# A PEER layer on Trainium2: 128 of 512 tokens take their experts by indirect row loads

## The chip, the cores and the metric

The kernel runs on one core of a Trainium2 chip, as one launch. Its time is the device time of that core in microseconds, the median of several runs. The core's engines work side by side, each through its own list of instructions in order: TensorE (PE) for matmuls, VectorE (DVE) for element-wise work, ScalarE (ACT) for activations and copies, GpSimd (POOL) for slower element-wise work and for indirect DMAs, SyncE (SP), which only issues DMAs here. Semaphores join them.

## The reference, cut to what matters

Two transformer blocks in float32, model width 1024. In the first block each of 2 layers has a mixer and then a PEER layer; layer 0 runs PEER on 256 tokens of `x` and 256 of `ctx` (512), layer 1 on 256. A token scores two sets of 128 sub-keys for each of 8 heads, keeps the best 16 of each, and of the 256 sums the best 16: 128 experts a token, out of 16384. The second block (2 layers of feed-forward, mixer, feed-forward on 256 tokens) follows.

```python
s = einsum('chpd,hpnd->chpn', q, sub_keys); s_top, i_top = top_k(s, 16)
cand = s_top[:, :, 0, :, None] + s_top[:, :, 1, None, :]      # and ids i*128 + j
best, pos = top_k(cand, 16); eid = take(cand_id, pos); gate = softmax(best)
u = take(u_tab, eid)                                          # rows of 1024
act = gelu(einsum('chkd,cd->chk', u, hc)) * gate
v = take(v_tab, eid)
return einsum('chk,chkd->cd', act, v)
```

## The kernel before

PEER is computed densely: every token is multiplied with all 16384 rows of the u-table, and all entries but a token's 128 get the gate 0. Both tables come as 128 **pieces** of 128 x 1024 floats (512 KB): SP loads one into `raw` (4 buffers), ACT copies it to `wh` in the fp32r format (L338), and DVE subtracts to get the rest `wl` (L339); where `self.share` is set, every third piece of layer 0 has that subtraction on POOL. A product is three matmuls, wh·xh, wh·xl, wl·xh (`mm3`, L370 to L372), so a piece costs 24 matmuls of 128 x 128 weights against all 512 tokens.

`peer(0)` has two stages. In the **up stage** the u-pieces run through PE (`ublock`, 4 pieces a block), ACT applies gelu (L1169), and the result goes to DRAM (`ad`). Woven into it, `topk` chooses the experts, a tile of 128 tokens after the other: scores on PE (L987), top 16 on DVE (L995 to L999), the candidates' top 16 (L1031 to L1035), 128 selecting steps `cj` (L1050), and then the gates are spread over the 16384 columns by one-hot matrices: `oa` and `ob` on DVE (L1085, L1095), a matmul into `sc` (L1106), an ACT copy (L1111), a POOL addition into `stg` (L1113), a DMA to `gd`. A loop hands `topk` 3.5 units of budget for each u-piece.

In the **down stage** `prep` loads a block of gates and of activations (`g`, `a`, 1 MB each, L1206 and L1211), DVE multiplies them (L1215) and splits them (`w4h`, `w4l`), and the v-pieces multiply them, in 16 groups of two blocks with 8 outputs `d` each; `ev` (L1222) adds the output from PSUM to the residual `xt` on DVE, 128 times. After each `ev` one `sums_step` (L432) prepares a modulation row of later layers: a 512 KB load `arow` and a DVE pass over 128 x 1024 that sums (L442). 48 rows `wmodt` (16 of them are summed twice) and 72 rows `adat` are treated here. `bias_write` (L1398) writes a table `dd` by two DMAs that POOL issues. Layer 1 repeats both stages on 256 tokens, with groups of four blocks and no sums.

A scheduler simulates the program and sets each engine's order from priorities; `topk` runs at a raised one. So the order is not written in the code but follows from it.

## Time and profile before

| | |
|---|---|
| median of 3 runs | 4311.34 us (4310.23 to 4319.42) |
| profiled execution | 4310.78 us |
| its span | 4308.9 us |
| granted TensorE clock, mean | 0.969 |
| busy: PE, DVE, ACT, POOL | 94%, 71%, 43%, 16% |
| up stage of layer 0 | 517 to 1333 us |
| down stage of layer 0 | 1333 to 2084 us |
| up and down stage of layer 1 | 2356 to 2772, 2772 to 3187 us |

The busy share tells how long an engine held an instruction, averaged over stages that have different limits. So the table gives the stretches of the four PEER stages, and the rows further down give what each engine does in each of them. In a timeline the engine's instructions overlap a little at their ends; the distance from start to start is what one more of them costs.

### The profile page before, as it was taken

What the parts mean: (1) busy time and instruction counts of PE and PEld (TensorE: products, weight loads), DVE (VectorE), ACT (ScalarE), POOL (GpSimd) and SP (SyncE); (2) the same over time, 40 slices, a digit from 0 to 9 for tenths busy, and PEclk for the clock granted to TensorE, in tenths of its full rate; (3) what the DMA queues carried; (4) which work ended last, traced back from release to release, by engine and by line L of the source; (5) the groups of instructions that cost most, each with busy time, mean ns of one, the idle gap of its engine ahead of it and who ended that gap; (6) DMA issues with size and microseconds to landing.
All of it is one profiled execution on the core that took longest, in us unless ns stands there. A gap on an engine that the chain in (4) does not pass through costs nothing.

```text
span 4308.9 us, 68836 instructions
## 1 busy us (share of the span) xinstructions
PE 4066.0 (94%) x25534; PEld 3593.9 (83%) x25534; DVE 3048.2 (71%) x7720; ACT 1851.1 (43%) x3052; POOL 690.5 (16%) x612
## 2 busy tenths in 40 slices
PE   7899999999997899999988999999989989999898
PEld 5568788888885688888768999999989879998798
DVE  4754586878776887787676989676658778656764
ACT  3342344444443232322344565544444454444643
POOL 0100024333342000000020476400000110101100
PEclk9999999999998999999999999999999999999999
DMA  5423246454559988786324577887659628564344
GB/s 175 164 72 98 93 134 194 158 184 147 187 171 233 312 291 295 278 299 216 104 65 167 191 259 239 280 308 260 223 178 313 214 94 288 178 195 152 99 161 142
DMA packets 309551, 841.63 MB, mean 195 GB/s; under 512 B 26672, under 2 KB 130736, under 8 KB 296672
## 3 DMA queue, kind: packets, MB, share of 16 engines
q1 hardware_dynamic: 200480, 735.51, 50.0%
q10 hardware_dynamic: 107328, 98.57, 7.0%
q0 software_dynamic: 1408, 3.15, 1.1%
q8 instruction: 202, 3.31, 0.3%
q14 instruction: 133, 1.09, 0.1%
HBM read 734.38 MB, written 102.75 MB: 194 GB/s over the span
## 4 chain that ended last, share of the span: by engine, by line
PE 51%; issue 7%; DVE 7%; DMA 2%; ACT 1%; POOL 1%; ACTq 0%; DVEq 0%; POOLq 0%
PE mm L370 16%; PE mm L371 16%; PE mm L372 16%; DMA a<-ad 2%; DVE wl L339 1%; DVE cj L1050 1%; PE sc L1106 1%; DVE cacc L769 0%; ACT wh L338 0%; DVE nu L534 0%; PE sc L509 0%; PE sc L698 0%; PE nm L708 0%; ACTq L1192 0%; DVE a L1215 0%
## 5 line engine op out<-in xcount | busy, mean ns | idle before, releaser
L338 ACT ACTIVATE wh<-raw 128x1024 fp32r<-128x1024 f32 x946 | 999.6, 1058 | 1819.1 <-PE mm L371 1377.8
L339 DVE TENSOR_TENSOR wl<-raw,wh 128x1024 fp32r<-128x1024 f32 x839 | 1042.9, 1246 | 596.0 <-ACT wh L338 594.4
L372 PE MATMUL mm<-h2h,wl 128*128 128x512 f32 (+1 forms) x2176 | 736.0, 339 | 6.2 <-DVE wl L339 6.1
L370 PE MATMUL mm<-h2h,wh 128*128 128x512 f32 (+1 forms) x2176 | 733.5, 338 | 2.7 <-ACT h2h L539 2.2
L371 PE MATMUL mm<-h2l,wh 128*128 128x512 f32 (+1 forms) x2176 | 735.6, 338 | 0.0
L370 PE MATMUL mm<-w4h,wh 128*128 128x512 f32 (+1 forms) x2048 | 691.6, 340 | 36.5 <-ACT wh L338 18.8
L371 PE MATMUL mm<-w4l,wh 128*128 128x512 f32 (+1 forms) x2048 | 690.5, 339 | 4.1 <-DVE w4l L339 4.1
L372 PE MATMUL mm<-w4h,wl 128*128 128x512 f32 (+1 forms) x2048 | 662.6, 339 | 4.1 <-DVE wl L339 4.0
L370 PE MATMUL mm<-h,wh 128*128 128x256 f32 x1712 | 498.7, 291 | 16.5 <-ACT h L539 6.7
L371 PE MATMUL mm<-h,wh 128*128 128x256 f32 x1712 | 494.6, 289 | 2.4 <-DVE h L540 1.8
L372 PE MATMUL mm<-h,wl 128*128 128x256 f32 x1712 | 491.0, 287 | 0.5 <-DVE wl L339 0.5
L370 PEld LDWEIGHTS mm<-w4h,wh 128*128 128x128 f32 x2048 | 391.8, 192 | 84.9 <-ACT wh L338 27.2
L372 PEld LDWEIGHTS mm<-h2h,wl 128*128 128x128 f32 x2176 | 414.4, 191 | 48.8 <-DVE wl L339 9.4
L370 PEld LDWEIGHTS mm<-h2h,wh 128*128 128x128 f32 x2176 | 414.5, 191 | 45.3 <-ACT h2h L539 2.8
L371 PEld LDWEIGHTS mm<-h2l,wh 128*128 128x128 f32 x2176 | 414.7, 191 | 40.6
L371 PEld LDWEIGHTS mm<-w4l,wh 128*128 128x128 f32 x2048 | 392.1, 192 | 47.2 <-DVE w4l L339 6.5
L372 PEld LDWEIGHTS mm<-w4h,wl 128*128 128x128 f32 x2048 | 388.9, 192 | 47.7 <-DVE wl L339 7.4
L1095 DVE SCALAR_TENSOR_TENSOR ob<-io,top,ix 128x256 fp32r<-128x256 f32 x768 | 322.3, 475 | 145.9 <-PE sc L1106 144.7
L370 PEld LDWEIGHTS mm<-h,wh 128*128 128x128 f32 x1712 | 335.8, 196 | 24.4 <-ACT h L539 10.7
L1113 POOL TENSOR_TENSOR stg<-s 128x256 f32<-128x256 f32 x384 | 312.6, 844 | 228.4 <-ACT s L1111 220.1
L339 POOL TENSOR_TENSOR wl<-raw,wh 128x1024 fp32r<-128x1024 f32 x107 | 263.1, 2459 | 505.7 <-ACT wh L338 444.7
L371 PEld LDWEIGHTS mm<-h,wh 128*128 128x128 f32 x1712 | 335.4, 196 | 9.8 <-DVE h L540 7.1
(339 smaller groups left out, 6809.0 us busy)
## 6 DMA issues: line engine op xcount, KB each, us to landing
raw<-in_ut SPq DMA_DIRECT2D x256, 512.0 KB, 3.9
raw<-in_vt SPq DMA_DIRECT2D x256, 512.0 KB, 4.9
raw<-in_wgu SPq DMA_DIRECT2D x176, 512.0 KB, 4.3
arow<-in_adat SPq DMA_DIRECT2D x144, 512.0 KB, 4.9
gd<-stg ACTq DMA_DIRECT2D x24, 2048.0 KB, 11.2
raw<-in_wdn SPq DMA_DIRECT2D x88, 512.0 KB, 4.3
raw<-in_win SPq DMA_DIRECT2D x66, 512.0 KB, 3.7
ad<-a ACTq DMA_DIRECT2D x32, 1024.0 KB, 4.2
```

The lines of the kernel that those rows point to most:

```text
L338: self.nc.scalar.activation(h, src, AF.Copy)
L339: (eng or self.nc.vector).tensor_sub(l, src, h.bitcast(F32))
L370: mm(out, wh, xh, start=start, stop=False)
L371: mm(out, wh, xl, start=False, stop=False)
L372: mm(out, wl, xh, start=False, stop=stop)
L1050: nc.vector.scalar_tensor_tensor(junk, self.iota[:, :NCAND], pf[:, h, k : k + 1], eid[:, h, :], op0=OP.is_equal, op1=OP.mult, accum_out=se ...
L1095: nc.vector.scalar_tensor_tensor(ob[:, j], iota.unsqueeze(1).to_broadcast([P, 2, P]), ij[:, 1, t : t + 1], ghl[:, t].unsqueeze(2).to_broad ...
L1106: nc.tensor.matmul(pg[:, j * 256 : (j + 1) * 256], oa[:, 2 * h + j], obs[h][:, j].rearrange("p a b -> p (a b)"), start=True, stop=True,)
L1113: nc.gpsimd.tensor_tensor(stg[:, :, c : c + 2].rearrange("p b t -> p t b"), both[:, :, 0], both[:, :, 1], op=OP.add)
```

## The change

Of layer 0, tile 0 (the first 128 tokens, `rows_at(0)`) no longer goes through the dense passes. Its `topk` stops once the expert ids and gates are known (`keep`): the one-hot part is made for three tiles only. 128 **indirect loads** on POOL's queue (`fetch`: each takes, for each of 128 tokens, the 4 KB row of one of its experts, 512 KB in all) bring u-rows into 3 buffers `ur`, and a DVE pass over 128 x 1024 multiplies each with the tokens' input, transposed into PSUM (`xg`), and sums (`rows_up`, 1.17 rows a u-piece once the ids are there). In the down stage 128 more loads bring v-rows into 4 buffers `vr`, each scaled and added to `racc` by one DVE pass (`rows_down`, 1.15 rows an `ev`); at the end 8 PE transposes put the sum into `xt`. The dense matmuls of layer 0, `gd`, `ad` and the steps on them run on `nd` = 384 columns.

With it go: PSUM buffers `mm` 4 to 2 (the transposed input takes two banks); the sub-keys, no longer resident, are loaded as two `raw` pieces for each `topk` tile; the budget 3.5 becomes 3.05; the u-loop of layer 0 runs all 32 blocks in the up stage; the 72 `adat` sums move from the down stage of layer 0 to that of layer 1 (1.25 for each of its 64 `ev`), and the 48 `wmodt` rows stay at 0.42 an `ev`.

```diff
-    a["sk"] = sk.reshape(L, P, 8, 256)
+    a["sk"] = sk.reshape(L, P, 2, 8, P).transpose(0, 2, 1, 3, 4)
+    a["ug"], a["vg"] = i["u_tab"][0], i["v_tab"][0]
...
-    rate = {("gate", 0): (10, 0, 2), ("gate", 1): (4, 0, 2), ("u", 0): 0, ("u", 1): 0, ("v", 0): 1, ("v", 1): 0, "ffn": 1.4, "out": 1, "att": (0.4, 0.4), "norm": ((4,4), (2,2), (4,4), (4,4))}
-
-
-    def topk(self, l, tt, tp, qT, sk, gd):
+    rate = {("gate", 0): (10, 0, 2), ("gate", 1): (4, 0, 2), ("u", 0): 0, ("u", 1): 0, ("v", 0): 0.42, ("v", 1): 1.25, "up": 1.17, "down": 1.15, "ffn": 1.4, "out": 1, "att": (0.4, 0.4), "norm": ((4,4), (2,2), (4,4), (4,4))}
...
+            if hp % 2 == 0:
+                sk = self.raw(self.A["sk"][l, hp // 2]).rearrange("p (a b) c -> p a (b c)", a=4)
...
+        if keep is not None:
+            nc.vector.tensor_copy(keep["id"], sel.rearrange("p h k -> p (h k)"))
+            nc.vector.tensor_copy(keep["gate"], gate.rearrange("p h k -> p (h k)"))
+            keep["ready"] = True
+            return
...
+    def rows_at(self, l):
+        return P if l == 0 else 0
+    def fetch(self, pool, tag, bufs, table, ids, i):
+        r = self.t(pool, [P, D], tag, bufs=bufs)
+        self.nc.gpsimd.indirect_dma_start(
+            out=r, out_offset=None, in_=self.A[table], in_offset=bass.IndirectOffsetOnAxis(ap=ids[:, i : i + 1], axis=0)
+        )
+        return r
+    def rows_up(self, pool, dst, x):
+        todo = []
+        for i in range(P + 2):
+            if i < P:
+                todo.append(self.fetch(pool, "ur", 3, "ug", dst["id"], i))
+            if i >= 2:
+                r = todo.pop(0)
+                self.nc.vector.scalar_tensor_tensor(
+                    r, r, 1.0, x, op0=OP.mult, op1=OP.mult, accum_out=dst["dot"][:, i - 2 : i - 1]
+                )
+                yield
+        a = dst["dot"]
+        self.nc.scalar.activation(a, a, AF.Gelu_apprx_tanh)
+        self.nc.vector.tensor_tensor(a, a, dst["gate"], op=OP.mult)
+    def rows_down(self, pool, dst, acc):
+        todo = []
+        for i in range(P + 3):
+            if i < P:
+                todo.append(self.fetch(pool, "vr", 4, "vg", dst["id"], i))
+            if i >= 3:
+                r = todo.pop(0)
+                c = dst["dot"][:, i - 3 : i - 2]
+                if i == 3:
+                    self.nc.vector.tensor_scalar(acc, r, c, None, op0=OP.mult)
+                else:
+                    self.nc.vector.scalar_tensor_tensor(acc, r, c, acc, op0=OP.mult, op1=OP.add)
+                yield
...
-            es.enter_context(self.banks(mm=4, sc=3, io=1))
+            es.enter_context(self.banks(mm=2 if g0 else 4, sc=3, io=1))
...
+                if g0:
+                    rhs = (lambda k: h2h[:, k, g0:], lambda k: h2l[:, k, g0:])
+                    x = self.t(self.psum, [P, D], "xg", bufs=1)
+                    for k in range(8):
+                        for n, h in enumerate((h2h, h2l)):
+                            nc.tensor.matmul(
+                                x[:, k * P : (k + 1) * P], h[:, k, 0:g0].bitcast(F32), self.ident, start=n == 0, stop=n == 1
+                            )
...
-                while not done and nb < 32:
+                while nb < 32 and not (done and not g0):
...
+                        if g0 and "ready" in dst:
+                            if up is None:
+                                up = self.rows_up(tp, dst, x)
+                                steps = 0
+                            steps += self.rate["up"]
+                            while steps >= 1:
+                                steps -= 1
+                                next(up, None)
...
+                for _ in up or ():
                     pass
...
-                        cols = slice(s * T, s * T + T)
+                        cols = slice(max(g0, s * T), s * T + T)
                         add = nc.vector.scalar_tensor_tensor(
-                            self.xt[:, d, cols], ps[:, cols], mod[:, 40 + d, s : s + 1], self.xt[:, d, cols],
+                            self.xt[:, d, cols], ps[:, cols.start - g0 : cols.stop - g0], mod[:, 40 + d, s : s + 1], self.xt[:, d, cols],
...
+                    if g0:
+                        self.steps += self.rate["down"]
+                        while self.steps >= 1:
+                            self.steps -= 1
+                            with self.tc.issue_after(add.ins):
+                                next(down, None)
...
-                        vp, 4, (0, 1, 2),
-                        (*self.sums_of("wmodt", 0, self.mod1[1], "b_mod1", lambda m: (0, 1) if m < 16 else (0,)),
-                         *self.sums_of("adat", 0, self.mod2[0], "ada_b0", lambda m: (2,))),
+                        vp, 4, (0, 1), self.sums_of("wmodt", 0, self.mod1[1], "b_mod1", lambda m: (0, 1) if m < 16 else (0,))
                     )
+                else:
+                    self.sums_begin(vp, 3, (2,), self.sums_of("adat", 0, self.mod2[0], "ada_b0", lambda m: (2,)))
+                if g0:
+                    acc = self.t(vp, [P, D], "racc")
+                    down = self.rows_down(vp, dst, acc)
+                    self.steps = 0
...
+                    if g0 and i + deep == 32:
+                        rows_end()
...
-                            self.mm3(ps[:, :nt], wh, wl, gh[:, kk], gl[:, kk], k == 0, k == 4 * deep - 1)
-                        ev(d, ps[:, :nt], i + deep == 32)
+                            self.mm3(ps[:, :nd], wh, wl, gh[:, kk], gl[:, kk], k == 0, k == 4 * deep - 1)
+                        ev(d, ps[:, :nd], i + deep == 32)
...
-        self.peer(0, 3.5)
+        self.peer(0, 3.05)
```

Three places of the order. First VectorE, where the selection of tile 0 ends in the up stage (`cj` is the last selecting step; `si`, `idx`, `pf`, `best` lead into the one-hot part; `rowid` holds the ids), before:

```order
L1050 SCALAR_TENSOR_TENSOR cj_1047_4924,sel_894_4475<-io_774_3646,pf_893_4473,eid_875_4311 128x50
L339 TENSOR_TENSOR wl_942_4592<-raw_940_4589,wh_941_4591 128x1024
L1057 CAST si_1048_4926<-sel_894_4475 128x128
L1060 TENSOR_SCALAR idx_1049_4928<-si_1048_4926 128x128
L1061 TENSOR_SCALAR idx_1049_4928<-si_1048_4926 128x128
L1064 CAST pf_1050_4931<-idx_1049_4928 128x128
L1065 CAST best_1051_4932<-idx_1049_4928 128x128
L1085 TENSOR_TENSOR oa_1062_4980<-io_774_3646,top_1053_4939 128x512
L1075 TENSOR_TENSOR ix_1055_4942<-sc_1052_4935,gh_1054_4941 128x128
L1095 SCALAR_TENSOR_TENSOR ob_1063_4982<-io_774_3646,top_1053_4939,ix_1055_4942 128x256 x2
L1095 SCALAR_TENSOR_TENSOR ob_1064_4985<-io_774_3646,top_1053_4939,ix_1055_4942 128x256 x2
L1085 TENSOR_TENSOR oa_1065_4988<-io_774_3646,top_1053_4939 128x512
```

and now:

```order
L1053 SCALAR_TENSOR_TENSOR cj_1061_5012,sel_903_4529<-io_774_3646,pf_902_4527,eid_884_4365 128x50
L1060 CAST rowid_775_3651<-sel_903_4529 128x128
L1151 SCALAR_TENSOR_TENSOR ur_1075_5081,rowdot_777_3653<-ur_1075_5081,xg_841_4013 128x1024
L340 TENSOR_TENSOR wl_1024_4888<-raw_1022_4885,wh_1023_4887 128x1024
L1151 SCALAR_TENSOR_TENSOR ur_1076_5083,rowdot_777_3653<-ur_1076_5083,xg_841_4013 128x1024
L1151 SCALAR_TENSOR_TENSOR ur_1077_5085,rowdot_777_3653<-ur_1077_5085,xg_841_4013 128x1024
L340 TENSOR_TENSOR wl_1045_4954<-raw_1043_4951,wh_1044_4953 128x1024
L1151 SCALAR_TENSOR_TENSOR ur_1082_5135,rowdot_777_3653<-ur_1082_5135,xg_841_4013 128x1024
L1151 SCALAR_TENSOR_TENSOR ur_1087_5185,rowdot_777_3653<-ur_1087_5185,xg_841_4013 128x1024
L998 MAX top_1073_5069<-s_1066_5048 128x8 x8
```

Where the one-hot steps followed, 128 row passes begin, right behind the ids; a `wl` stands between them, and the selection of the next tile begins with the MAX row.

Second GpSimd, where the up stage ends and the down stage begins, before:

```order
L1113 TENSOR_TENSOR stg_2525_11640<-s_2410_11098 128x2x128 x9
L1113 TENSOR_TENSOR stg_2583_11916<-s_2410_11098 128x2x128 x16
L1398 DMA dd_2888_13732<-bv0_2890_13735 1024x1x383
L1398 DMA dd_2888_13732<-bv1_2892_13740 1024x1x383
L846 MEMSET u_3507_17737 128x2x15
```

and now:

```order
L1121 TENSOR_TENSOR stg_2537_11674<-s_2345_10779 128x2x128 x16
L1138 DMA vr_2652_12252<-in_vg,rowid_775_3651 128x1024
L1138 DMA vr_2653_12254<-in_vg,rowid_775_3651 128x1024
L1138 DMA vr_2654_12256<-in_vg,rowid_775_3651 128x1024
L1138 DMA vr_2655_12258<-in_vg,rowid_775_3651 128x1024
L1495 DMA dd_2867_13585<-bv0_2869_13588 1024x1x383
L1495 DMA dd_2867_13585<-bv1_2871_13593 1024x1x383
L1138 DMA vr_2657_12288<-in_vg,rowid_775_3651 128x1024
L1138 DMA vr_2666_12332<-in_vg,rowid_775_3651 128x1024
L1138 DMA vr_2668_12362<-in_vg,rowid_775_3651 128x1024
L1138 DMA vr_2677_12406<-in_vg,rowid_775_3651 128x1024
```

The two writes of `dd` now have four loads of v-rows ahead of them and the other 124 behind them on one queue.

Third VectorE in the middle of the down stage, where before the sums `arow` fill the places between the `ev` (L1222):

```order
L1222 SCALAR_TENSOR_TENSOR xt_4_72<-mm_2923_13960,mod1_0_12_87,xt_4_72 128x256 x2
L442 SCALAR_TENSOR_TENSOR arow_2912_13885,mod1_1_13_88<-arow_2912_13885,crow0_2655_12305 128x1024
L1222 SCALAR_TENSOR_TENSOR xt_4_72<-mm_2931_14003,mod1_0_12_87,xt_4_72 128x256 x2
L442 SCALAR_TENSOR_TENSOR arow_2920_13927,mod1_1_13_88<-arow_2920_13927,crow0_2655_12305 128x1024
L339 TENSOR_TENSOR wl_2947_14091<-raw_2945_14088,wh_2946_14090 128x1024
L448 TENSOR_TENSOR mod1_1_13_88<-mod1_1_13_88,vecs_2_67 128x4
L339 TENSOR_TENSOR w4l_2939_14054<-a4_2940_14055,w4h_2938_14053 128x512 x4
L1215 TENSOR_TENSOR a4_2984_14363<-a4_2984_14363,g4_2981_14359 128x512 x4
L339 TENSOR_TENSOR wl_2954_14145<-raw_2952_14142,wh_2953_14144 128x1024
L1222 SCALAR_TENSOR_TENSOR xt_4_72<-mm_2941_14069,mod1_0_12_87,xt_4_72 128x256 x2
```

and now:

```order
L340 TENSOR_TENSOR wl_2910_13830<-raw_2908_13827,wh_2909_13829 128x1024
L1292 SCALAR_TENSOR_TENSOR xt_4_72<-mm_2897_13754,mod1_0_12_87,xt_4_72 128x128
L1292 SCALAR_TENSOR_TENSOR xt_4_72<-mm_2897_13754,mod1_0_12_87,xt_4_72 128x256
L1170 SCALAR_TENSOR_TENSOR racc_2625_12132<-vr_2884_13673,rowdot_777_3653,racc_2625_12132 128x1024
L1292 SCALAR_TENSOR_TENSOR xt_4_72<-mm_2905_13796,mod1_0_12_87,xt_4_72 128x128
L1292 SCALAR_TENSOR_TENSOR xt_4_72<-mm_2905_13796,mod1_0_12_87,xt_4_72 128x256
L1170 SCALAR_TENSOR_TENSOR racc_2625_12132<-vr_2892_13715,rowdot_777_3653,racc_2625_12132 128x1024
L340 TENSOR_TENSOR wl_2913_13848<-raw_2911_13845,wh_2912_13847 128x1024
L340 TENSOR_TENSOR wl_2930_13943<-raw_2928_13940,wh_2929_13942 128x1024
L340 TENSOR_TENSOR w4l_2921_13906<-a4_2922_13907,w4h_2920_13905 128x384 x2
```

A row pass stands where the sum stood; `ev` adds the second half of `x` and all of `ctx` (128 and 256 columns).

## Rows read from the trace of the kernel before

**Rows 1.** Chain that ended last: share of the span by engine

```profile
PE 51%; issue 7%; DVE 7%; DMA 2%; ACT 1%; POOL 1%; ACTq 0%; DVEq 0%; POOLq 0%
```

**Rows 2.** Windows: PE, PEld, DVE, ACT, POOL busy (instructions); clock, DMA share, GB/s

```profile
517.00:1333.00 816.00, 806.61 (x3771) 672.64 (x3769) 616.92 (x2634) 358.34 (x564) 298.27 (x298) 1.00 0.52 171
1333.00:2084.00 751.00, 712.45 (x3058) 577.79 (x3059) 571.46 (x953) 210.82 (x272) 2.55 (x4) 0.97 0.80 267
...
2772.00:3187.00 415.00, 411.42 (x3404) 411.02 (x3403) 282.14 (x465) 196.59 (x292) 0.00 (x0) 0.99 0.71 249
```

**Rows 3.** Timeline, TensorE, up stage: start, length, instruction; 17 steps apart

```profile
1295.74 0.39 PE L371 MATMUL mm<-h2l,wh 128*128 128x512 f32 x1
...
1299.59 0.39 PE L370 MATMUL mm<-h2h,wh 128*128 128x512 f32 x1
```

**Rows 4.** The same in layer 1, 256 tokens; 29 steps apart

```profile
2959.72 0.28 PE L371 MATMUL mm<-w4l,wh 128*128 128x256 f32 x1
...
2963.20 0.28 PE L371 MATMUL mm<-w4l,wh 128*128 128x256 f32 x1
```

**Rows 5.** Groups by line, up stage: busy us, mean ns, idle before, releaser

```profile
L1095 DVE SCALAR_TENSOR_TENSOR ob<-io,top,ix 128x256 fp32r<-128x256 f32 x512 | 215.5, 476 | 137.7 <-PE sc L1106 137.3
L339 DVE TENSOR_TENSOR wl<-raw,wh 128x1024 fp32r<-128x1024 f32 x92 | 121.9, 1325 | 43.6 <-ACT wh L338 43.6
L1106 PE MATMUL sc<-ob,oa 128*128 128x256 f32 x512 | 87.1, 287 | 3.9 <-DVE ob L1095 2.6 <-ACT s L1111 1.2
L1169 ACT ACTIVATE a<-mm 128x512 f32<-128x512 f32 x128 | 74.3, 580 | 3.5 <-PE mm L372 3.4
```

**Rows 6.** Timeline, VectorE, a one-hot group in the up stage

```profile
700.60 0.68 DVE L1085 TENSOR_TENSOR oa<-io,top 128x512 fp32r<-128x512 f32 x1
701.20 1.65 DVE L1095 SCALAR_TENSOR_TENSOR ob<-io,top,ix 128x256 fp32r<-128x256 f32 x4
702.76 0.68 DVE L1085 TENSOR_TENSOR oa<-io,top 128x512 fp32r<-128x512 f32 x1
```

**Rows 7.** Timeline, VectorE, down stage of layer 0

```profile
1462.84 1.21 DVE L339 TENSOR_TENSOR wl<-raw,wh 128x1024 fp32r<-128x1024 f32 x1
1463.98 0.86 DVE L1222 SCALAR_TENSOR_TENSOR xt<-mm,mod,xt 128x256 f32<-128x256 f32 x2
1464.76 0.15 DVE L448 TENSOR_TENSOR mod<-mod,vecs 128x8 f32<-128x8 f32 x1
1464.84 1.21 DVE L442 SCALAR_TENSOR_TENSOR arow<-arow,crow 128x1024 f32<-128x1024 f32 x1
1465.98 0.07 DVE L442 DVE_READ_ACCUMULATOR arow<-arow,crow 128x1 f32 x1
```

**Rows 8.** GpSimd's groups of both stages, 400 to 2400 us

```profile
L1113 POOL TENSOR_TENSOR stg<-s 128x256 f32<-128x256 f32 x256 | 197.9, 802 | 207.9 <-ACT s L1111 199.9 <-issue 7.9
L339 POOL TENSOR_TENSOR wl<-raw,wh 128x1024 fp32r<-128x1024 f32 x51 | 128.1, 2512 | 373.8 <-ACT wh L338 314.5 <-PE sc L1106 56.8 <-PE mm L371 2.5
L1398 POOL DMA_DIRECT2D dd<-bv x2 | 2.4, 1183 | 24.7 <-ACT bv L1397 24.7
```

**Rows 9.** DMA, 1450 to 2050 us: queue, packets, MB, share of 16 engines; an issue

```profile
q1 hardware_dynamic: 38834, 166.58, 79.1%
raw<-in_vt SPq DMA_DIRECT2D x110, 512.0 KB, 4.9
```

**Rows 10.** DMA, 1318 to 1450 us: 40 slices, software queue, issues' median us to landing

```profile
GB/s 377 331 305 312 379 338 258 164 429 402 430 401 425 301 133 96 114 121 95 71 83 90 94 96 94 123 120 139 116 232 310 396 395 418 413 418 420 416 407 389
q0 software_dynamic: 1408, 3.15, 36.4%
a<-ad SPq DMA_DIRECT2D x7, 1024.0 KB, 15.0
dd<-bv POOLq DMA_DIRECT2D x2, 1532.0 KB, 65.8
```

**Rows 11.** Chain of waits in the same stretch

```profile
1374.94 48.01 DMA a<-ad
```

More of the change, by code (lines that the diff above doesn't have):

```diff
@@ L987, in topk @@
                 nc.tensor.matmul(
-                    ps[:, j * 256 : (j + 1) * 256], qT[:, 2 * hp + j, cols], sk[:, 2 * hp + j, :], start=True, stop=True
+                    ps[:, j * 256 : (j + 1) * 256], qT[:, 2 * hp + j, cols], sk[:, 2 * (hp % 2) + j, :], start=True, stop=True
                 )
@@ L1117, in late @@
                         nc.scalar.dma_start(
[L1118 removed]
+                            gd[:, :, (tt - self.rows_at(l) // P) * 4 + g].rearrange("b a c -> a b c"), stg.rearrange("a (b q) c -> a b (q c)", q=4)
                         )
@@ L1137, in peer @@
             pp = es.enter_context(self.pool(f"pp{l}"))
+            up = None
+            if g0:
+                dst = {n: self.t(pp, [P, P], f"row{n}", t) for n, t in (("id", I32), ("gate", F32), ("dot", F32))}
             hes = es.enter_context(ExitStack())
@@ L1175, in tk @@
                     for tt in range(nt // P):
-                        yield from self.topk(l, tt, tp, qT, sk, gd)
+                        yield from self.topk(l, tt, tp, qT, gd, dst if tt * P < g0 else None)
                 tg = tk()
@@ L1194, in peer @@
                 for _ in tg:
+                    pass
+                for _ in up or ():
                     pass
```

43 lines of the change are left out of this document (29 added, 14 removed).

## The prediction

> **What bounds the kernel now.** I read the chain of waits first: by engine it is PE, 51% of the span, and DVE, 7%, the rest being small [rows 1]. A share of the whole span mixes stages, so next come the windows of the PEER stages [rows 2], and they differ. In the up stage of layer 0 PE is busy for 807 of 816 us at a granted clock of 1.00 and DVE for 617: PE is the bound, DVE has 199 us free, the DMA engines half. In the down stage PE is busy for 712 of 751 at 0.97, DVE for 571, and the DMA share is 0.80: PE is the bound again, but DMA is not far behind. The down stage of layer 1 has PE at 411 of 415, DVE at 282 and a DMA share of 0.71. The reader is to see two things: what is taken from PE in layer 0 is worth something only until DVE or DMA is last, and each stage needs its own sum. Then the groups and timelines give the price of one instruction.
>
> **The change on PE.** With 512 tokens 17 matmuls take 1299.59 − 1295.74 = 3.85 us, 0.2265 us each [rows 3]; with 256 tokens 29 take 3.48 us, 0.120 each [rows 4]. 384 columns don't occur; I take the middle, 0.173, since the step from 256 to 512 costs nearly in proportion to the columns. The bounds are 0.120 and 0.2265. Each stage has 128 pieces of 24, 3072 matmuls: 696 us before, 532 after. In the up stage PE's other work was 807 − 696 = 111, of which the 512 one-hot matmuls [rows 5] are 61 at 0.12; 384 stay, 46. So PE comes to 532 + 46 + 50 = 628 there, and to 532 in the down stage, 712 − 532 = 180 less.
>
> **DVE in the up stage.** Of the 617 us, one-hot: `ob` has a pitch of 1.56/4 = 0.39, `oa` of 0.60 [rows 6]; 512 x 0.39 + 128 x 0.60 = 277. `wl`: 92 [rows 5], a start-to-start of 1.14 in a quiet place [rows 7], and a mean of 1.325 here, 0.11 more than in that quiet place (1.21); I take 1.23, 113 us. The selection is what is left, 617 − 277 − 113 = 227 for four tiles. After: one-hot 3/4 of 277, 208; selection still 227; `wl` 86 (42 of the 128 u-pieces stand on POOL in the new order), 106. The row passes are new: 128 over 1024 elements. `arow` is the same operation from SBUF, 1.14 [rows 7]; the input is read from PSUM here, and an element-wise step on 256 elements from PSUM costs 0.39 [rows 6] against 0.34 for 256 at the SBUF slope, (1.14 − 0.60)/512 per element and 0.06 fixed; with 0.05 for that and 0.01 to 0.07 for the accumulator's read [rows 7], 1.25 each, 160 us. Sum 208 + 227 + 106 + 160 = 701: DVE overtakes PE (628) and sets the stage. A DVE that never waits gives 701; adding the wait for the first row, `wl` and `ob` that wait for ACT and PE for a while (182 us of idle before them in the old stage [rows 5], most of it because PE was late, which it no longer is), I take 735. **Gain 81**, bounds 115 and 30.
>
> The Trainium skill (SBUF — State Buffer, section "SBUF: two separate sides") says that a DVE instruction with two SBUF inputs and a GpSimd instruction that reads SBUF block each other. The mean of `wl`, 1.325 us with POOL busy, fits that, and a row pass, which has one input in PSUM, would by it be spared; were it slowed as `wl` is, the stage would be 14 us longer.
>
> **What hides the rest of the up stage.** POOL: `stg` 192 x 0.80, `wl` 42 x 2.5, and 128 gathers at the 1.18 that an issue of `dd` held it [rows 8], 154 + 105 + 151 = 410 of 735. With `mm` halved to two buffers, the gelu of a piece (0.58 on ACT [rows 5]) must be done while PE computes the next one, 24 x 0.173 = 4.2 us; if ACT's queue lost that cover, 128 x 0.58 = 74 us at most, and PE has 107 free. The sub-keys are two loads of 512 KB a tile, 8 in all, among 128 pieces. The 16 transposes of the input are 2 us of PE. I cost these at nothing.
>
> **The down stage.** DVE: `wl` 127 x 1.14 = 145; the 48 `wmodt` rows are 64 sums of 1.15, 74, and 2 for the additions; `ev` 128 x (0.39 + 0.26) = 83; `prep` 256 steps on 384 elements, 0.60 − 0.13 = 0.47 each, 121; `rows_down` 128 x 1.14, 146; some 12 others: 583. DMA: v-pieces 67 MB, v-rows 67, gates 25, activations 25 (each 3/4 of 33.5), `wmodt` 25, together 209 MB. From before, 166.58 MB took 79.1% of 600 us of engine time, 2.85 us a MB [rows 9]; but loads in the stretch before reach 420 GB/s in a slice, 2.38 us a MB [rows 10]. So 498 to 596 us, and on top `dd`: 36.4% of 132 us, 48, in which the others fall to about 100 GB/s [rows 10]; the chain has 48 us on the load of one block of activations there [rows 11]. DMA therefore 546 to 644, DVE 583, PE 532: three resources nearly level, DVE and DMA above PE. The v-rows behind `dd` on POOL's queue come late in that stretch, and DVE's fifth row pass waits, with `wl` and so PE behind it; before, that stretch was already lost, so I add 40 to DVE, not more, and 17 for the first `prep`. Levelled resources never overlap wholly: 583 + 57 = 640 and DMA's 644 give 665. **Gain 86**, bounds 130 and 30.
>
> **The down stage of layer 1.** It takes the 72 `adat` sums: DVE 282 + 72 x 1.15 = 365 of 415, DMA 103 + 38 = 141 MB, 336 to 402. PE stays the bound at 411 but loses its reserve. Bounds 0 and +45; I take **+20**, since the stage ran at a DMA share of 0.71 and now comes near that of the old down stage (0.80), where PE lost 39 us of 751 [rows 2].
>
> **Sum.** The profiled execution took 4310.8 us, 1.9 more than its span and within 1 us of the median, so no correction: 4310.8 − 81 − 86 + 20 = **4164**.
>
> **Rivals.** *Rows come late in the up stage (the slower side).* Three buffers hold three rows, each from its issue to the end of its DVE pass. If a gather needs L us from issue to landing, 128 rows need 128 x (L + 1.25)/3. The order puts them over 90 pieces, about 90 x 5.75 = 517 us, so L up to 11 costs nothing; the gain of 147 is used up at L = 14.3, since a late row holds up DVE and with it `wl` and PE. At 16, 736 − 517 = 219 are lost: **4383**. For it: `dd`, the only DMA of that queue, took 65.8 us, and a 1 MB load 15.0 beside it [rows 10]. Against: 512 KB loads take 4.9 [rows 9], and `dd` is 1.5 MB in packets of 2.2 KB written to DRAM.
>
> The Trainium skill (DMA: Bandwidth & Descriptors, section "Anatomy of one DMA — SWDGE (gpsimd) path") fits a DMA from GpSimd by 2.0 us and its bytes over 436 GB/s: for 512 KB an estimate of 3.2 us. No row here shows it; by it this rival falls.
>
> *Gathered bytes are dearer for the DMA engines.* At 1.5 times the price of a piece, 33.5 MB more in effect: 80 to 95 us in the down stage, which is at its DMA limit, nothing in the up stage: **4250**. At twice, 160 to 190 there and some 30 in the up stage, where DMA's 0.52 x 816 = 424 would become about 765: **4366**, slower. `dd` speaks for it: 48 us for 3.15 MB are 15 us a MB [rows 10], five times a piece's price; against it, a row is 4 KB in one run, as a partition of a piece is.
>
> *DVE's work is hidden* in both stages (row passes in places where PE waits anyway, the rest as PE gives): up 645, down 600, layer 1 +0: **3990**. Against it, DVE's own sums of 701 and 583.
>
> *384 columns cost as much as 512.* Then PE keeps 807 − 15 and 712 us and the change gives back its small gain in layer 1: **4310**. Against it, 256 columns take 0.53 of 512's time [rows 3, 4].
>
> **How the numbers follow.** Forecast 0.71; late rows 0.08; dearer bytes 0.10 at about 1.5 times and 0.04 at twice; hidden DVE 0.04; no cheaper matmul 0.03. Runs of this kernel can tell 0.2% from no change, 9 us. Faster: forecast, 1.5 times, hidden DVE, 0.85. Same: 0.03. Slower: late rows and twice, 0.12. The bounds of the three terms, −115 to −30, −130 to −30 and 0 to +45, don't fall on one side together; taken as independent they make about ±80 round 4164. The range reaches from 4075 to 4290, which takes in dearer bytes at 1.5 times and leaves out late rows, twice, hidden DVE and no cheaper matmul, 0.19.
>
> **What the new profile would show.** Right: a pitch of 0.173 for matmuls on 384 columns; in the up stage DVE nearly always busy and PE waiting for `wl` and `ob`; row passes of 1.2 us that begin without a wait for the gathers; in the down stage a DMA share over 0.9 and PE at about 0.8, a wait for v-rows right behind `dd`; the down stage of layer 1 near 435. Wrong: idle time of DVE that ends with `ur` or `vr` in the middle of a stage (late rows, or bytes that cost more, told apart by the queue's share of engine time against its bytes), PE still over 95% busy in layer 0, or a down stage of layer 1 beyond 460.

## The result and the profile after

The changed kernel takes 4217.6 us (median of 4 runs, 4216.7 to 4220.8), the kernel before 4314.6 (median of 4); ratio 0.9776, 95% interval 0.9759 to 0.9793. It is faster by 97 us where 147 were forecast, and lies within the stated range. The profiled execution took 4220.8 us with a span of 4219.0, 90 less than the span before.

Where the 90 lie shows when each stage is timed by its own ends in TensorE's timeline: the first matmul of layer 0's PEER (495.3 us in both), the last one-hot matmul, the last matmul of the v-pieces, and so on; "rest" is all that follows layer 1's down stage.

| us | before | after | moved | forecast |
|---|---|---|---|---|
| up stage, layer 0 | 835.1 | 796.7 | −38 | −81 |
| down stage, layer 0 | 758.1 | 696.0 | −62 | −86 |
| mixer, layer 1 | 274.1 | 275.4 | +1 | 0 |
| up stage, layer 1 | 373.9 | 373.4 | −1 | 0 |
| down stage, layer 1 | 451.2 | 456.3 | +5 | +20 |
| rest | 1121.3 | 1125.9 | +5 | 0 |

The windows of the kernel after, with the columns of [rows 2] (PE, PEld, DVE, ACT and POOL busy, clock, DMA share, GB/s): the up stage, its last 55 us alone, the down stage in three parts, the down stage of layer 1.

```profile
517.00:1292.00 775.00, 690.82 (x3658) 654.42 (x3656) 689.99 (x2727) 319.06 (x498) 383.73 (x360) 0.92 0.73 250
1237.00:1292.00 55.00, 41.06 (x107) 28.29 (x105) 54.49 (x127) 31.63 (x54) 38.43 (x52) 0.55 0.59 182
1292.00:1430.00 138.00, 72.92 (x327) 67.27 (x327) 67.87 (x111) 28.42 (x42) 23.86 (x20) 0.72 0.94 244
1430.00:1930.00 500.00, 446.57 (x2427) 428.65 (x2426) 482.92 (x753) 150.24 (x205) 163.19 (x114) 0.97 0.93 345
1930.00:1988.00 58.00, 57.99 (x335) 57.67 (x333) 37.35 (x69) 19.06 (x28) 0.00 (x0) 1.00 0.38 124
2637.00:3093.10 456.10, 449.11 (x3703) 445.14 (x3701) 374.68 (x640) 212.09 (x319) 14.06 (x8) 1.00 0.92 336
```

TensorE no longer fills either stage of layer 0. In the up stage VectorE is busy for 690 of 775 us; the sum had said 701. In the down stage it is busy for 588 (583 in the sum): half idle at the start, 97% in the middle, and for 37 of the last 58 us, which TensorE fills at full clock. So VectorE's work was sized rightly. What was not is the time in which VectorE waits: 85 us in the up stage and 108 in the down stage, against 34 and some 82 allowed.

Who waited for whom in the up stage (VectorE's list, then TensorE's; us, times, longest):

```profile
DVE ur L1151 <- DMA ur<-in_ug,rowid: 38.2, 22, 6.4
DVE wl L340 <- ACT wh L339: 20.3, 11, 4.8
DVE ob L1103 <- PE sc L1114: 10.0, 7, 3.5
...
PE mm L373 <- DVE wl L340: 34.5, 17, 7.0
PE mm L371 <- ACT a L1229: 16.0, 14, 6.0
PE sc L1114 <- DVE ob L1103: 13.1, 24, 1.8
```

The largest is what the late-rows rival named: 22 of 128 passes wait for their row. And in the down stage (TensorE's list):

```profile
PE mm L371 <- DVE xt L1292: 53.7, 41, 6.4
PE mm L373 <- DVE wl L340: 24.4, 5, 14.1
PE mm L371 <- ACT wh L339: 20.9, 9, 13.2
PE mm L371 <- ACT w4h L339: 18.0, 2, 16.2
```

The first line is a wait that the kernel before does not have in the down stage: TensorE waits for `ev`, the addition that empties its output buffer. TensorE's three longest before the change:

```profile
PE mm L370 <- ACT wh L338: 18.8, 4, 8.5
PE mm L370 <- ACT w4h L338: 17.4, 1, 17.4
PE mm L372 <- DVE wl L339: 4.0, 4, 2.7
```

### The profile page after: what moved, and what is told of

It reads as the page before. It is cut to its first block, busy times and chain, and to the rows that moved or that the text cites. A ratio compares the mean times of both kernels' runs of the same rounds, so it can differ in the third digit from the quotient of the medians.

```text
span 4219.0 us, 69354 instructions
## 1 busy us (share of the span) xinstructions
PE 3821.8 (91%) x25443; PEld 3558.0 (84%) x25443; DVE 3217.7 (76%) x7949; ACT 1792.4 (42%) x2986; POOL 959.9 (23%) x804
## 3 DMA queue, kind: packets, MB, share of 16 engines
q0 software_dynamic: 38272, 137.38, 10.2%
## 4 chain that ended last, share of the span: by engine, by line
PE 37%; DVE 7%; issue 7%; DMA 1%; ACT 1%; POOL 1%; ACTq 0%; POOLq 0%; DVEq 0%; SPq 0%
PE mm L371 11%; PE mm L373 11%; PE mm L372 11%; DVE wl L340 2%; DVE cj L1053 1%; PE sc L1114 1%; DMA raw<-in_vt 1%; ACT wh L339 1%; DVE cacc L770 0%; DVE nu L535 0%; PE sc L510 0%; PE sc L699 0%; PE nm L709 0%; ACTq L1260 0%; PE sc L495 0%
## 5 line engine op out<-in xcount | busy, mean ns | idle before, releaser
L371 PE MATMUL mm<-w4h,wh 128*128 128x384 f32 (+1 forms) x2048 | 642.7, 317 | 95.0 <-DVE xt L1292 53.7
L373 PE MATMUL mm<-h2h,wl 128*128 128x256 f32 (+2 forms) x2176 | 689.3, 318 | 39.3 <-DVE wl L340 37.7
L371 PE MATMUL mm<-h2h,wh 128*128 128x256 f32 (+2 forms) x2176 | 689.4, 318 | 25.6 <-ACT a L1229 16.0
L372 PE MATMUL mm<-h2l,wh 128*128 128x256 f32 (+2 forms) x2176 | 687.6, 316 | 0.0
L373 PE MATMUL mm<-w4h,wl 128*128 128x384 f32 (+1 forms) x2048 | 620.1, 315 | 29.3 <-DVE wl L340 29.1
L372 PE MATMUL mm<-w4l,wh 128*128 128x384 f32 (+1 forms) x2048 | 637.8, 314 | 1.2 <-DVE w4l L340 1.2
L371 PEld LDWEIGHTS mm<-h,wh 128*128 128x128 f32 x1712 | 337.0, 197 | 23.9 <-ACT h L540 10.2
L373 PEld LDWEIGHTS mm<-h,wl 128*128 128x128 f32 x1712 | 336.2, 197 | 0.7 <-DVE wl L340 0.7
L1121 POOL TENSOR_TENSOR stg<-s 128x256 f32<-128x256 f32 x320 | 266.8, 858 | 93.8 <-ACT s L1119 86.7
```

Source lines behind the costliest of these rows:

```text
L371: mm(out, wh, xh, start=start, stop=False)
L372: mm(out, wh, xl, start=False, stop=False)
L373: mm(out, wl, xh, start=False, stop=stop)
L1121: nc.gpsimd.tensor_tensor(stg[:, :, c : c + 2].rearrange("p b t -> p t b"), both[:, :, 0], both[:, :, 1], op=OP.add)
```

## The experiments

My theory after the two traces: VectorE is the bound of both stages of layer 0 (A for the up stage, E for the down stage), and what is missing went into its waits for rows and, at the start of the down stage, for what stands behind `dd` (D). The rivals: TensorE's lower granted clock is a cause and not a consequence (B), the transfers crowd out the pieces, or the halved output buffers hold TensorE (F). G came later, on why `dd` costs what it costs.

Each is the changed kernel with one edit, unless it says more. Stage lengths are measured as in the table above, in one profiled execution each. Between kernels with the same code in the up stage that stage ran from 795 to 813 us, so less than some 18 us there means little.

**The rows apart.** Three kernels take the row work away, whole or by halves. The first has neither loads (`fetch` returns nothing) nor passes, the second has the loads but not the passes, which are left out like this in `rows_up` and likewise in `rows_down`:

```diff
-                self.nc.vector.scalar_tensor_tensor(
-                    r, r, 1.0, x, op0=OP.mult, op1=OP.mult, accum_out=dst["dot"][:, i - 2 : i - 1]
-                )
+                if i == 2:
+                    self.nc.vector.memset(dst["dot"], 0.0)
                 yield
```

The third has the passes and no loads (the passes of `rows_up` write to a spare tile, which is not shown). Each of the three ran once:

```diff
-        r = self.t(pool, [P, D], tag, bufs=bufs)
-        self.nc.gpsimd.indirect_dma_start(
-            out=r, out_offset=None, in_=self.A[table], in_offset=bass.IndirectOffsetOnAxis(ap=ids[:, i : i + 1], axis=0)
-        )
-        return r
+        if i == 0:
+            self.own = self.t(pool, [P, D], tag, bufs=1)
+            self.nc.vector.memset(self.own, 0.25)
+        return self.own
```

> The changed kernel without the row work: no indirect loads and no row passes in either stage (the first 128 tokens get no PEER output); everything else as changed. It gives the price of the rows as a whole. Theory A (VectorE is the bound and late rows make the rest): VectorE loses 164 us of busy time in the up stage, 690 - 164 = 526, so TensorE, 628 us of work at full clock, bounds it: up stage about 665 instead of 775-797 by its ends (495 to 1292). Down stage about 640 instead of 696, most of what stays being the start behind the dd write. Total about 4220 - 110 - 55 = 4055. Theory B (the lower granted clock of TensorE, 0.92 in the up stage, is the cause and not the rows): clock stays near 0.92 and the up stage stays above 730.

> The changed kernel with all 256 indirect loads but without the row passes on VectorE (the first 128 tokens get no PEER output). It prices the transfers and GpSimd's issues alone. Theory A: they cost little by themselves, up stage within 15 us and down stage within 20 us of the kernel without any row work, total about 4070. Rival (the transfers crowd out the pieces: DMA share 0.86 in the up stage, 0.93 in the down stage): the down stage stays near 690 and the total above 4130.

> The changed kernel with all 256 row passes but without the indirect loads: each pass reads one and the same resident tile (the first 128 tokens get a wrong PEER output). It takes away the lateness of rows and their DMA traffic and leaves VectorE's work. Theory A: the 38 us that VectorE waits for rows in the up stage go, and some more of what hangs on them, 797 - 45 = about 750; in the down stage the 18 us of waiting and part of the start go, 696 - 35 = 660; total about 4140. If the waits for rows were covered by other work anyway: up stage within 10 us of 797, total about 4190. If the rows' lateness and their traffic were all of the cost: total about 4060, as without rows.

| us | up | down | total |
|---|---|---|---|
| no rows | 654 | 641 | 4021.7 |
| indirect loads only | 680 | 700 | 4104.5 |
| passes only | 742 | 687 | 4149.0 |
| both (the change) | 797 | 696 | 4217.6 |

The windows of the up stage, in this order:

```profile
517.00:1148.40 631.40, 618.86 (x3608) 607.91 (x3607) 545.68 (x2467) 306.20 (x490) 271.78 (x231) 1.00 0.58 193
```

```profile
517.00:1173.00 656.00, 620.07 (x3535) 606.14 (x3534) 547.45 (x2464) 302.32 (x484) 392.68 (x359) 0.97 0.81 283
```

```profile
517.00:1233.40 716.40, 666.41 (x3644) 635.75 (x3642) 681.25 (x2715) 317.17 (x498) 258.68 (x233) 0.95 0.53 176
```

Without rows TensorE is the bound at a clock of 1.00, 619 us of 631: theory A's 665 was near (its total of 4055 was 33 too high, since 143 us left the up stage and not 110), and theory B (the clock by itself) falls. The clock follows: in these four up stages TensorE is idle for 13, 36, 50 and 84 us of the window and is granted 1.00, 0.97, 0.95 and 0.92. In the last 55 us of the changed kernel's up stage, where VectorE's one-hot steps set the pace, it is granted 0.55, near the lower of its two levels (1.2 of 2.4 GHz). The passes alone cost 88 us of the up stage, the loads alone 26 (15 at most by theory A), and both 143. So the loads are not free, as the sum had them: they cost 55 on top of the passes. The 29 that neither has alone are near the wait for late rows (38), which needs both; that they are this wait is argued and not shown.

In the down stage the passes are nearly all of it, 687 of 696 (theory A had expected 660), with the DMA share at 0.69 instead of 0.89: there VectorE and what hangs on it is the bound, and not the DMA engines. The loads alone came out at 700, against the 660 that theory A expected, and as the rival had it. In that kernel nothing paces the loads, and they run far ahead of the pieces: the last is issued 257 us before the stage ends, and until then the DMA share is 0.98 and more. There they do crowd out the pieces; in the changed kernel the passes pace them, so this number says little about it.

**More room for rows.** 4 buffers for u-rows and 7 for v-rows.

```diff
-                todo.append(self.fetch(pool, "ur", 3, "ug", dst["id"], i))
-            if i >= 2:
+                todo.append(self.fetch(pool, "ur", 4, "ug", dst["id"], i))
+            if i >= 3:
...
-                todo.append(self.fetch(pool, "vr", 4, "vg", dst["id"], i))
-            if i >= 3:
+                todo.append(self.fetch(pool, "vr", 7, "vg", dst["id"], i))
+            if i >= 6:
...
-    ob_bufs = (3, 4)
+    ob_bufs = (3, 3)
```

> The changed kernel with 4 instead of 3 buffers for u-rows (3 fetched ahead) and 7 instead of 4 for v-rows (6 ahead); for the room, 3 instead of 4 buffers ob. Theory A: the waits for rows in the up stage fall from 38 us to about 15, the up stage by some 15 us; in the down stage the two waits behind the dd write (18 us) go, but the wait for v-pieces takes their place there, gain 5 to 15; total about 4195. Rival (rows are late because GpSimd issues them late, not for want of buffers): no change, within 8 us of 4217.

4210.8 us, ratio 0.9761 (0.9744 to 0.9777), up 791, down 693. The wait for u-rows fell from 38 us (22 times) to 23 (11 times), on the way to theory A's 15, but its total of 4195 was not reached, and the measured one is within the 8 us of the rival. TensorE's wait for `ob`, which gave up a buffer, grew from 13 to 21 us. So more room makes fewer rows late; that the time saved comes back is not shown. In the down stage the waits for v-rows are gone, and TensorE's wait for `wh` grew from 21 to 49 us in their place. Where the rows are late is seen in VectorE's timeline of the changed kernel:

```profile
868.00 1.21 DVE L1151 SCALAR_TENSOR_TENSOR ur<-ur,xg 128x1024 f32<-128x1024 f32 x1
869.14 0.08 DVE L1151 DVE_READ_ACCUMULATOR ur<-ur,xg 128x1 f32 x1
869.14 1.21 DVE L1151 SCALAR_TENSOR_TENSOR ur<-ur,xg 128x1024 f32<-128x1024 f32 x1
...
871.85 1.20 DVE L1151 SCALAR_TENSOR_TENSOR ur<-ur,xg 128x1024 f32<-128x1024 f32 x1
...
878.50 1.22 DVE L1151 SCALAR_TENSOR_TENSOR ur<-ur,xg 128x1024 f32<-128x1024 f32 x1 [3.96 <-DMA ur<-in_ug,rowid]
...
881.93 1.22 DVE L1151 SCALAR_TENSOR_TENSOR ur<-ur,xg 128x1024 f32<-128x1024 f32 x1 [2.20 <-DMA ur<-in_ug,rowid]
```

Three passes that start within 4 us empty the three buffers; the refill takes a load's time, and the next pass waits with the `wl` behind it. The tile's summary gives that time, and the length of the passes (minimum, median, maximum):

```profile
L1138 POOL DMA_INDIRECT ur<-in_ug,rowid x128: 932/953/1992, 604.9 to 1095.8; - x128
L1151 DVE SCALAR_TENSOR_TENSOR ur<-ur,xg x128: 1190/1211/1223, 611.0 to 1104.4; 128x1024 f32<-128x1024 f32 x128
...
DMA to landing us min/median/max: 4.2/6.3/10.2
```

**Rows less dense**, by the rate at which they are written into the program:

```diff
-    "up": 1.17
+    "up": 1.0
```

> The changed kernel with 1.0 instead of 1.17 row passes for each u-piece, so that the rows reach into the last tile's selection and lie less densely before it. Theory A (22 rows are late because three buffers and 6 to 9 us from issue to landing need a row pass no more often than every 2.5 to 3 us, and the order bunches them): the wait for rows falls from 38 us to about 20, the up stage from 797 to about 780, total about 4200. Rival (DMA and GpSimd are too busy whatever the spacing): waits stay at 30 to 40, the up stage within 8 us of 797.

4216.5 us, up 800, waits for rows 37.8 us. This decides nothing: the scheduler put the rows where they had been (the last u-row pass at 1106 us, 1104 in the changed kernel), so the edit did not do what it was made for. Whether an even spacing would help stays open.

**The output buffers.** The change gives two PSUM banks of `mm` to the transposed input for the whole of `peer(0)`. Here they come back for the down stage.

```diff
-            es.enter_context(self.banks(mm=2 if g0 else 4, sc=3, io=1))
+            bes = es.enter_context(ExitStack())
+            bes.enter_context(self.banks(mm=2 if g0 else 4, sc=3, io=1))
...
+            if g0:
+                bes.close()
+                bes.enter_context(self.banks(mm=4, sc=3))
             with self.pool(f"vp{l}") as vp:
```

> The changed kernel with four instead of two PSUM buffers mm in the down stage (the two that held the transposed input are given back after the up stage). TensorE waits 54 us for ev (the addition from PSUM on VectorE, line 1292) in the down stage. Theory E (VectorE is the bound there, the wait for ev is how it shows): down stage gains at most 15 us, and another wait, for wl, takes its place. Rival F (the halved buffers are the cause, which was costed at nothing): 40 to 50 us less, down stage about 650, total about 4170.

4188.4 us, ratio 0.9706 (0.9690 to 0.9723); down 666, 30 less. TensorE's waits there:

```profile
PE mm L373 <- DVE wl L340: 47.0, 29, 14.4
PE mm L371 <- ACT wh L339: 29.3, 36, 13.0
PE mm L371 <- ACT w4h L339: 16.2, 1, 16.2
PE mm L371 <- DVE wl L340: 1.1, 4, 0.3
PE mm L371 <- DVE xt L1296: 0.5, 2, 0.3
```

The wait for `ev` is gone, 54 to 0.5, and about half of it came back as a wait for `wl`. The truth lies between the two: the buffers cost 30 us, more than theory E's 15, less than rival F's 40 to 50, since VectorE is close behind.

**The table dd.** It is made and written in the up stage of layer 1.

```diff
                 self.share = self.shares[l]
+                if l == 1:
+                    self.bias_write(tp, *self.bias_load(tp))
...
-                    if l == 0 and i == 8:
-                        self.bias_write(vp, *bias)
```

> The changed kernel with the table dd made and written in the up stage of layer 1 instead of at the start of the down stage of layer 0: its two writes no longer stand between the fourth and the fifth load of v-rows. Theory D (the start of the down stage is lost to dd on the DMA engines): of the 138 us between 1292 and 1430, in which TensorE has about 57 us of work, some 45 go; down stage 696 to about 650. In layer 1 the up stage, at a DMA share of 0.69, grows by 0 to 15. Total 4217 to about 4180. Rival (the start is lost to loads and splits that come late anyway): down stage above 685, total within 10 us of 4217 or above.

4204.9 us, ratio 0.9736 (0.9715 to 0.9758). Down stage 643.5, 52 less, as theory D has it; but the up stage of layer 1 went from 373 to 410. TensorE's longest wait there:

```profile
PE sc L990 <- DMA raw<-in_sk: 31.5, 1, 31.5
```

The sub-keys are no longer resident, and their load is what stood behind `dd`. So the start was lost to `dd`, and its place matters less than what must land in the 60 us after it.

**Both, with dd in the mixer of layer 1.** The edit of the output buffers, and `dd` here:

```diff
             with self.banks(mm=2, sc=2, tr=2, nm=1, ad=1), self.pool(f"ap{l}") as ap:
+                if l == 1:
+                    self.bias_write(ap, *self.bias_load(ap))
```

> The changed kernel with both: four PSUM buffers mm in the down stage again, and dd made and written in the mixer of layer 1 (which moves only 0.35 of the DMA engines' time) instead of at the start of the down stage of layer 0. Measured apart, the buffers gave 30 us of the down stage and dd's leaving 52, but in the up stage of layer 1 dd cost 37 again. If the two losses are separate: down stage 696 - 82 = about 615, close to VectorE's 588 us of work; mixer 275 to about 280; total 4217 - 75 = about 4140. If the same wait stood behind both: down stage about 640, total about 4165.

4162.6 us, ratio 0.9635 (0.9613 to 0.9657): the fastest of all. Down stage 613, VectorE busy for 585 of them:

```profile
1290.00:1903.70 613.70, 562.64 (x3081) 535.09 (x3080) 585.06 (x930) 196.83 (x274) 231.48 (x132) 0.98 0.92 342
1903.70:2215.40 311.70, 243.92 (x1596) 206.12 (x1596) 189.36 (x397) 121.86 (x227) 38.56 (x25) 0.88 0.49 112
```

The two losses are separate (82 together, 30 + 52 apart). The second line is the mixer, 312 instead of 275: `dd` costs 36 here too; the forecast of 280 was wrong, and with it the total of 4140. From 1915 to 1950 us `dd` has the DMA engines to itself (packets, MB, share of 16 engines):

```profile
q0 software_dynamic: 395, 1.82, 96.6%
```

These 1.82 MB in 35 us are all that moves, 52 GB/s; no other load gets a byte.

**dd in 16 pieces**, one head each, behind every eighth `stg` of layer 1's up stage, with four `mm` buffers:

```diff
-            nc.gpsimd.dma_start(
-                dd[8 * g : 8 * g + 8].rearrange("h (p w) -> h p w", w=SHIFT),
-                vv[:, 0:SHIFT].unsqueeze(1).to_broadcast([8, P, SHIFT]),
-            )
+            for h in range(8):
+                nc.gpsimd.dma_start(
+                    dd[8 * g + h : 8 * g + h + 1].rearrange("h (p w) -> h p w", w=SHIFT),
+                    vv[h : h + 1, 0:SHIFT].unsqueeze(1).to_broadcast([1, P, SHIFT]),
+                )
+                yield
...
+                    if l == 1 and q % 4 == 3:
+                        with self.tc.issue_after(put.ins):
+                            next(self.part, None)
```

> The changed kernel with four PSUM buffers mm in the down stage, and dd made in the up stage of layer 1 and written in 16 pieces (one head each, one behind every eighth addition stg on GpSimd) instead of two. dd cost 52 us at the start of the down stage of layer 0, 37 in one go in the up stage of layer 1 and 36 in the mixer. Theory G (it costs because its two writes fill the DMA engines for some 60 us on end, longer than the piece buffers last): spread out, each piece holds them for about 3 us, and the up stage of layer 1 grows by 0 to 12 (374 to about 380); mixer back at 276, down stage of layer 0 at 613; total 4163 - 30 = about 4132. Rival (its engine time is paid wherever it lies): up stage of layer 1 about 410, total about 4162.

4211.4 us (0.9758, 0.9741 to 0.9774): worse than in one piece. The up stage of layer 1 takes 434 us (375 with `dd` in the mixer), its down stage 469 (456). The DMA queues of 2195 to 2660 us show a piece of the price (queue, packets, MB, share of 16 engines):

```profile
q0 software_dynamic: 1024, 3.14, 18.4%
...
gd<-stg ACTq DMA_DIRECT2D x8, 2048.0 KB, 19.8
```

18.4% of 465 us are 86 us of all engines for the same bytes that took 48 in [rows 10]: theory G's forecast falls, and so does the rival's 4162. Most of the up stage's loss is one wait, for ACT's copies of `sc` (53 us, 6 in the changed kernel); the first line is TensorE's wait, the others are from ACT's timeline:

```profile
PE sc L1114 <- ACT s L1119: 52.9, 6, 11.0
...
2549.00 14.85 ACTq L1265 DMA_DIRECT2D ad<-a  x1
...
2563.89 0.60 ACT L1119 ACTIVATE s<-sc 128x512 f32<-128x512 f32 x1 [14.81 <-issue]
```

The eight writes of `gd` take 18 to 25 us to land (11 to 16 in the changed kernel), and the first write of `ad` behind each stands in ACT's queue, up to 14.9 us, with the copies behind it. The 28 `ad` writes of layer 1 hold that queue for 96 us, 27 in the changed kernel. So the smaller pieces were dearer and met another queue; whether spreading by itself would help stays open.

**VectorE's load in the down stage.** Two kernels: fewer row passes for each `ev`, so that they last longer, and every third `wl` of that stage on GpSimd.

```diff
-    "down": 1.15
+    "down": 1.05
```

```diff
-                self.share = 0
+                self.share = 3 if g0 else 0
             if nb == 32:
                 hes.close()
...
+                self.share = 0
                 self.sums_end()
```

> The changed kernel with 1.05 instead of 1.15 row passes for each ev of the down stage, so that they last nearly to the last group. Theory E (VectorE bounds the middle of the stage, 483 of 500 us busy, and then TensorE alone its last 58 us, in which VectorE has 21 us free): spreading the rows gives back 10 to 20 us of the down stage, 696 to about 680, total about 4203. Rival (the middle is bound by TensorE waiting for output buffers and weights, not by the sum of VectorE's work): no change within 8 us.

> The changed kernel with every third subtraction wl of the down stage of layer 0 on GpSimd, which has some 190 of 696 us busy there: VectorE loses about 42 x 1.14 = 48 us. Theory E (VectorE bounds the middle of the down stage): 696 to about 660, total about 4180. Rival (the DMA engines bound it, share 0.93): no gain, down stage 690 to 700. A loss is to be feared if GpSimd's queue, whose row loads wait for VectorE in order, holds the wl behind them: then down stage above 700 and TensorE waiting for wl of GpSimd.

With 1.05: 4225.1 us, ratio 0.9786 (0.9770 to 0.9802), down 700: no gain, and theory E's 10 to 20 us are not there. It came out as its rival had it, that the middle is held by TensorE's wait for output buffers: that wait is 60 us here. With `wl` on GpSimd: 4254.9, ratio 0.9853 (0.9837 to 0.9869), down 723: a loss. GpSimd's waits:

```profile
POOL vr L1138 <- DVE racc L1170: 256.5, 83, 20.5
POOL wl L340 <- ACT wh L339: 116.3, 22, 24.3
```

Its queue stands 256 us on row loads that wait for a buffer, with the `wl` behind them, as was feared; but TensorE waits only 13 us for `wl` of GpSimd, and 38 for those of VectorE. What weighs more is that the edit took no work from VectorE: with 42 `wl` fewer it is busy for 611 us, 23 more than in the changed kernel. Its row passes (ns, minimum, median, maximum), in the changed kernel and then here:

```profile
L1170 DVE SCALAR_TENSOR_TENSOR racc<-vr,rowdot,racc x127: 1273/1283/1305, 1322.4 to 1924.8; 128x1024 f32<-128x1024 f32 x127
L1170 DVE SCALAR_TENSOR_TENSOR racc<-vr,rowdot,racc x127: 1267/1274/3885, 1329.2 to 1987.6; 128x1024 f32<-128x1024 f32 x127
```

The 26 of them that lie beside a step of GpSimd take 2.41 us in the mean; of the others none takes over 1.29. The other steps with two inputs in SBUF show the same: in the mean `w4l` takes 0.67 us instead of 0.56, and the product of gates and activations 0.63 instead of 0.56. `ev`, with one input in PSUM, is not slowed (0.47 on 256 columns, 0.48 before). That less work on VectorE alone shortens the stage is thereby not shown; four buffers and no `dd` showed it from the other side, by bringing the stage to within 29 us of VectorE's sum.

**The sums put back** into the down stage of layer 0, one for each `ev`, 120 loads as before.

```diff
-                        vp, 4, (0, 1), self.sums_of("wmodt", 0, self.mod1[1], "b_mod1", lambda m: (0, 1) if m < 16 else (0,))
+                        vp, 4, (0, 1, 2),
+                        (*self.sums_of("wmodt", 0, self.mod1[1], "b_mod1", lambda m: (0, 1) if m < 16 else (0,)),
+                         *self.sums_of("adat", 0, self.mod2[0], "ada_b0", lambda m: (2,))),
...
-                else:
-                    self.sums_begin(vp, 3, (2,), self.sums_of("adat", 0, self.mod2[0], "ada_b0", lambda m: (2,)))
```

> The changed kernel with the 72 adat sums put back from the down stage of layer 1 into that of layer 0 (1 a step of ev, 120 loads in all), as before the change. Theory E (VectorE bounds the down stage of layer 0, 588 of 696 us busy, and in layer 1 the sums lie beside TensorE): the down stage of layer 0 grows by the sums' 82 us, less the 21 us that VectorE has free at its end, 696 to about 760; the down stage of layer 1 falls by 5 us, 456 to 451; total about 4275. Rival (the move bought little, since the DMA engines bound both stages alike): total within 15 us of 4217.

4265.4 us, ratio 0.9880 (0.9863 to 0.9896): down stage 750.5, 54 more (760 by theory E), with VectorE busy for 672; down stage of layer 1 449.8, 6 less. The move is worth 48 us of the 97. The edit adds 38 MB of loads to the stage as well, so it does not tell VectorE's share from that of the DMA engines.

## Why the prediction was right, point by point

The time fell inside the range because each of the three terms fell inside its bounds: 38 us of 30 to 115, 62 of 30 to 130, and +5 of 0 to 45. Both gains came out short of the value taken, the first close to its lower end, and the third made up for a part. The bound of each stage and the work behind it were right; the price of the waits was not, and the width of the range took that up.

**Matmuls on 384 columns: right.** 0.173 was taken. TensorE's timeline in the up stage (start, length, instruction; 11 steps apart) gives 1.90/11 = 0.173:

```profile
1229.84 0.33 PE L373 MATMUL mm<-h2h,wl 128*128 128x384 f32 x1
...
1231.74 0.33 PE L372 MATMUL mm<-h2l,wh 128*128 128x384 f32 x1
```

The kernel without rows has TensorE busy for 619 us in the up stage, where the sum had 628.

**The bound of the up stage: right; its length: short by 43.** VectorE did overtake TensorE, and its sum was 701 against 690 measured. (A row pass was put at 1.25 us and stands 1.14 from the next; the 0.60 behind that estimate's slope for SBUF is `oa`'s, which reads `io` in PSUM.) The step that failed is "I take 735": passes alone gave 716 in that window, so 735 was too long without loads and too short with them, where it was 775. The loads were costed at nothing but their issue and the first row. They cost 55 (797 − 742), of which 26 come without the passes too; the other 29 may be the late rows.

**The late-rows rival: the mechanism was there, at another price.** VectorE idle until `ur` lands, in the middle of a stage, was on the prediction's list of signs that it is wrong, and 38 us of it are in the trace. "L up to 11 costs nothing" took the rows as evenly spaced. L was 6.3 in the median and at most 10.2, below that point, and yet 22 rows were late, since the order bunches them: what decides is not the mean distance of 4 us but the 4 us in which three passes stand.

**Dearer bytes: refuted.** In the up stage of the kernel after (517 to 1292 us):

```profile
q1 hardware_dynamic: 21140, 77.49, 29.0%
q0 software_dynamic: 18432, 67.12, 25.8%
```

29.0% of 775 us for 77.49 MB are 2.90 us a MB, 25.8% for 67.12 MB are 2.98: a gathered row costs what a piece costs. The Trainium skill's fit (DMA: Bandwidth & Descriptors, section "Anatomy of one DMA — SWDGE (gpsimd) path") gives an estimate of 3.2 us for 512 KB. Every gathered load of the trace took longer, 4.2 at the least; other traffic lay beside all of them, and no run here has one alone. By the Trainium skill (SBUF — State Buffer, section "SBUF: two separate sides") a VectorE instruction with two SBUF inputs and a GpSimd instruction that reads SBUF block each other. The traces agree: the passes of the up stage, with one input in PSUM, were not slowed: the 64 that lie beside an element-wise step of GpSimd take 1.21 us like the other 64. Those of the down stage, with two inputs in SBUF, went from 1.28 to 2.41 us beside GpSimd's `wl`.

**The down stage: VectorE's sum right, the gain 24 short.** VectorE's 583 came out as 588, the DMA engines' 546 to 644 as 619 (0.89 of 696), and TensorE's 532 as 577 busy at a granted clock of 0.93. The step that failed is in the paragraph on what hides: the halved `mm` was weighed for the up stage (gelu on ACT) and "costed at nothing"; for the down stage, where VectorE empties the buffers, it was not weighed at all. It cost 30 there. `dd` was named and priced at 40 for VectorE's fifth pass; taking it away gave 52. Its waits are in VectorE's list of the down stage, the longest 17.0 us for that row and 14.1 for a block of activations:

```profile
DVE a L1285 <- DMA a<-ad: 24.4, 4, 14.1
DVE racc L1170 <- DMA vr<-in_vg,rowid: 18.4, 2, 17.0
```

The prediction took the 100 GB/s of [rows 10] for the rate of the other loads; it is that of all traffic, and from 1366 to 1410 us of that trace `dd` has half of the bytes (2.27 MB against 2.21) and 88% of the engines' time. Of the three levelled resources the DMA engines were not one: passes without loads left the stage within 9 us.

**The moved sums: right in direction, cheaper.** +5 instead of +20 in layer 1: TensorE stayed busy for 449 of 456 us at a DMA share of 0.92, which the forecast took for a loss.

**Hidden VectorE and no cheaper matmul:** refuted by VectorE's 690 of 775 and the pitch of 0.173.

## What to carry to other kernels

Sum each engine's work by stage, and then ask separately for the waits: here VectorE's sums held within 2%, and nearly the whole miss lay in waits. Work moved from VectorE to GpSimd is to be checked on what it leaves: row passes of VectorE with two inputs in SBUF took nearly twice their time beside it. A buffer count that is halved has to be weighed in every stage that uses it, by the engine that empties it there. For a ring of loads, the time from issue to landing is to be set against the closest run of consumers in the order, not against their mean distance.
